# Zero products without pauses, and weight low parts on VectorE or GpSimd, in a two-layer hybrid backbone

## The chip, the cores and the metric

The kernel runs on one core of a Trainium2 chip. TensorE (PE) multiplies, VectorE (DVE), ScalarE (ACT) and GpSimd (POOL) do the elementwise work, and SyncE (SP) issues most transfers. The metric is the device time of one execution in microseconds: the median of several runs. Times below come from the runs and the profile of the kernel before.

## The reference

Two layers over 256 latent and 256 context tokens of width 1024, in fp32. Each layer: a modulated RMSNorm, one input projection for three mixers, a gated merge, an output projection, then a squared-ReLU MLP of width 4096. Cut to its core:

```python
for l in range(DEPTH):                       # DEPTH = 2
    sh1, sc1, g1, sh2, sc2, g2 = jnp.split(m_lat, 6, axis=-1)   # cond @ w_mod + b_mod
    h_lat = modulate(rmsnorm(x, norm1_g[l]), sh1, sc1)
    h_ctx = modulate(rmsnorm(ctx, norm1_g[l]), csh1, csc1)
    a_lat, a_ctx = parallel_mixer(h_lat, h_ctx, w_in[l], ...)   # GQA, neighbourhood, MLA
    x = x + g1 * a_lat
    x = x + g2 * sq_relu_mlp(modulate(rmsnorm(x, norm2_g[l]), sh2, sc2), w_mlp1[l], w_mlp2[l])
    if with_ctx:                             # layer 0 only
        ctx = ...                            # the same for the context tokens
return rmsnorm(x, final_norm_g)
```

In the mixer `ya`, `yb`, `yc` are softmax attentions over latent and context keys (8 heads of 64 each; the second with a 2-D window and a learned bias, the third with a low-rank key and a rotary part), and the merge is `(gates0 * (ya @ w_o_gqa) + gates1 * (yb @ w_o_na) + gates2 * (yc @ w_o_mla)) @ w_out`.

## The kernel before

**Split products.** Every fp32 product is three TensorE products of a reduced fp32 form: an operand a is split into hi (a cast on ScalarE, L723 for weights, L832 for activations) and lo = a - hi (a subtraction on VectorE, L724 and L833), and hi x hi + hi x lo + lo x hi goes into one PSUM bank (L786 to L788). A weight tile is 128 x 1024 fp32 (512 KB). Its fp32 form lands in a "raw" buffer (three of them, more while free slots are lent), ScalarE and VectorE write its pair wh, wl (three pairs, more when lent), and the raw buffer is given back when the low part is done. So a tile's low part sets when the next transfer into that buffer starts and when the third of its products may run. With 512 columns (layer 0: latent and context tokens) a tile carries 24 products of 512 columns, in layer 1 mostly 24 of 256.

**The order of the work.** While the program is built, a small event-driven planner plays it through. Each piece of work is a thread that asks for an engine with a cost, a lent buffer, an event or a sleep; each engine takes the waiting request with the lowest key, and the instruction is written into that engine's queue at that moment. An engine executes its queue in that order on the chip, waiting on semaphores. So the costs in the planner set only the order. The threads of the dense work come from a table of words (`SEQ`, one string a layer: `k0` is a weight tile of the keys, `gN2` a gate tile, `w` a tile of the modulation weights, `at` the square roots and rotations of the GQA queries and keys). The table also sets the order of the weight transfers. A request may name two engines ("any"); the first that is free takes it. `COLD` is the time up to which the planner doubles TensorE's costs and takes a longer transfer latency.

**The start.** The input is loaded, its squares are summed (ScalarE L983, VectorE L988), a product with ones gives the sums over channels (L1005), ScalarE takes the root (L1013), VectorE the reciprocal (L1014), a product spreads it over rows (L1026), and VectorE scales the input chunk by chunk (L1129). Meanwhile the conditioning weights arrive as sixteen tiles (c0 to c7, two halves each): four concurrent products of 32 columns a call (L859), a copy (L865), a sum over groups (L869) and two small VectorE steps (L876, L878). Then ScalarE modulates a chunk (L1137) and it is split (L832, L833).

**Attention.** Scores go to a bank, VectorE takes the row maximum (L1720, L1707), ScalarE the exponential (L1727), VectorE the reciprocal (L1739); the scaling is an "any" request of VectorE (L1738) and ScalarE (L1736); TensorE transposes (L1756), the result is split, and TensorE multiplies with the values (L1790, L1791). GpSimd issues the bias transfers (L1633) and clears and copies the rotary rows (L1463, L1469). Beside this the dense products of later tiles go on. The root of the GQA norms is L1524; the table for it and the table for the exponential are loaded in turn.

**Zeros.** `keep_warm` puts products of a zero tile (L914, 256 columns) into TensorE's queue where the planner sees TensorE idle.

Of the kernel before, what the change touches and what calls it, by code (L numbers as in the profile page):

```python
# [64 lines left out]

BR = {"N": NA, "L": ML, "G": GA}
SEQ = (
# [7 lines left out]
)  # L75


# [205 lines left out]
SL_W, SL_E, SL_G = 0.5, 10.0, 13.0  # L283
SL_M = 15.0
ANY = True
COLD = 9.0
IDLE = 0.08


# [247 lines left out]
def v_(n):  # L537
    return 0.07 + n * 0.00104
# [28 lines left out]
class Prog:  # L567
# [146 lines left out]
    def arrive(self, i, r, n):  # L714
        nc = self.nc
        yield from self.transfer(n)
        if self.keys[i][0] in ("mod", "modc"):
            self.raws[i] = r
            self.set("w", i)
            return  # L720
        pair = yield ("get", self.split, None)
        hi, lo = pair[0], pair[1]
        yield from self.act(n, lambda: nc.scalar.copy(hi[:, :n], r[0][:, :n]), SL_W)  # L723
        yield from self.dve(n, lambda: nc.vector.tensor_tensor(lo[:, :n], r[0][:, :n], hi[:, :n].bitcast(F32),  # L724
                                                               ALU.subtract), SL_W)
        self.give_raw(r)
        self.spl[i] = pair
        self.set("w", i)
# [177 lines left out]
    def keep_warm(self):  # L906

        nc, pl = self.nc, self.pl
        yield ("sleep", 2.0)
        while not self.ending and pl.now < 2000:  # L910
            if pl.busy["pe"] <= pl.now - IDLE and not pl.pend["pe"] and self.banks.free:
                def fn():
                    if self.banks.free:
                        nc.tensor.matmul(self.banks.free[0].ap[:, 0:256], self.zero,  # L914
                                         self.zero[:, 0:1].broadcast_to([P, 256]), start=True, stop=True)
                yield ("pe", 0.112, fn)
            else:
                yield ("sleep", 0.1)

    def cond_ready(self):  # L920
        yield ("sleep", 4.6)
# [716 lines left out]
    def attend(self, l, mine):  # L1638
        units = [(u, br, u % 4) for u, br in enumerate(b for b in BRANCHES for _ in range(4))]
        job = 0  # L1640
        for u, br, p in units:
            for e in sum(self.unit_needs(l, br, p), []):
                yield from self.wait(*e)
            yield from self.wait("ys", l, br)
            if u == 0:
                self.banks.caps.update(ATTN_CAPS)
                self.window.cap = WINDOW[1]
            kq, kv = self.unit_needs(l, br, p)
            groups = [(s, True) for s in range(2)] + ([(s, False) for s in range(2)] if l == 0 else [])
            nj = sum(2 if lat else 1 for s, lat in groups)  # L1650

            qleaf = []
            for e in kq:
                units_of = 4 if e[0] == "gak" else 1
                v = self.qk[e]
                if e not in self.leafs:
                    self.leafs[e] = Leaf(self, units_of * nj, [(self.arena, x) for x in v])
                qleaf.append(self.leafs[e])
            vleaf = []
            for e in kv:  # L1660
                if e not in self.leafs:
                    self.leafs[e] = Leaf(self, (4 if br == GA else 2) * len(groups), [(self.arena, self.vals[e])])
                vleaf.append(self.leafs[e])
            left = [len(groups)]
            for s, lat in groups:
                g = dict(u=u, br=br, p=p, s=s, lat=lat, n=2 if lat else 1, ready=Event(), got=Event(),
                         vleaf=vleaf, left=left)
                for qt in range(2 if lat else 1):
                    self.pl.spawn(self.job(l, g, qt, qleaf), job, -1)
                    job += 1  # L1670
                self.pl.spawn(self.pv(l, g), job - 0.5, -1)
        yield from self.wait("ydone", l, 11)
        self.free(*mine)
        self.banks.caps.update(DENSE_CAPS)
        self.window.cap = WINDOW[2]
        self.pl.serve(self.banks)
        self.pl.serve(self.window)
# [508 lines left out]
    def build(self, es):  # L2186
# [19 lines left out]
        self.wm_done, self.wm_total = 0, sum(i[0] == "wm" for i in self.items)  # L2206
        self.pl.busy["hw"] = 0.55
        self.pl.at(0.55, lambda: None)
        self.ending = False
        self.spawn(self.keep_warm(), 1 << 20, 9)  # L2210
        self.spawn(self.cond_ready(), 0)
        self.spawn(self.dense(), 0)
# [75 lines left out]
```

## Time and profile before

| | |
|---|---|
| median of 3 runs | 1442.91 us (1442.81 to 1444.1) |
| profiled execution | 1443.08 us, span 1441.3 us |
| busy: PE, DVE, ACT, POOL | 1417.8, 1074.0, 768.7, 52.9 us |
| granted TensorE clock | 0.994 of full, mean |
| transferred | 207.71 MB |
| zero products (L914) | 55 |

A line of the profile's groups reads: line, engine, operation, output <- inputs with their shapes, count, then busy time and mean length, then the idle time of that engine just before them and what ended it. A line of the order of time reads: start, length, engine, line, operation, names, count, and in brackets the idle time before it. A matmul's length overlaps the next one's, so TensorE counts as busy in the shadow of the last product too.

### The profile page before, as it was taken

How to read it: one execution, taken by the hardware profiler on the slowest of the kernel's cores; microseconds unless marked ns; L12 is line 12 of the kernel's file. 1: busy time of each engine (PE TensorE's matmuls, PEld its weight loads, DVE VectorE, ACT ScalarE, POOL GpSimd, SP SyncE). 2: the span in 40 equal slices, each digit the busy share in tenths (PEclk: the TensorE clock that was granted, in tenths of full speed). 3: DMA queues.
4: the chain of work that ended last, by engine and by line, in shares of the span. 5: the costliest groups of instructions: out<-in, count | busy, mean ns of one | idle time of the engine just before them, and what ended most of it. 6: DMA issues, size and time to landing. Idle time of an engine off the chain costs nothing.

```text
span 1441.3 us, 23357 instructions
## 1 busy us (share of the span) xinstructions
PE 1417.8 (98%) x8965; PEld 1268.1 (88%) x8965; DVE 1074.0 (75%) x2215; ACT 768.7 (53%) x1404; POOL 52.9 (4%) x91
## 2 busy tenths in 40 slices
PE   7999999999999999999999999999999999999997
PEld 4899889988888899888888889998998999999996
DVE  5638987859997779889867447657988997765555
ACT  6638886547842243413223234447779784554453
POOL 0000420000000000000000000000320000000000
PEclk8999999999999999999999999999999999999999
DMA  9501331413245444455655434334354427455551
GB/s 370 196 23 48 82 87 59 162 59 103 73 154 197 132 151 142 146 192 190 203 191 190 160 100 156 126 94 141 107 167 157 147 85 233 138 192 188 190 189 45
DMA packets 60528, 207.71 MB, mean 144 GB/s; under 512 B 7168, under 2 KB 8704, under 8 KB 60416
## 3 DMA queue, kind: packets, MB, share of 16 engines
q1 hardware_dynamic: 56448, 197.94, 41.3%
q0 software_dynamic: 2816, 6.82, 1.9%
q8 instruction: 70, 1.15, 0.3%
q10 hardware_dynamic: 1152, 1.45, 0.3%
q14 instruction: 42, 0.34, 0.1%
HBM read 201.47 MB, written 1.05 MB: 141 GB/s over the span
## 4 chain that ended last, share of the span: by engine, by line
PE 86%; DVE 7%; ACT 5%; DMA 1%; issue 1%; SPq 0%; DVEq 0%; ACTq 0%
PE b L786 25%; PE b L787 25%; PE b L788 25%; PE b L1756 2%; PE b L1791 2%; PE b L1790 2%; PE b L1584 1%; ACT s L1727 1%; PE b L1585 1%; DMA raw<-in_wts_dram 1%; ACT s L832 1%; DVE s L833 1%; DVE wl L724 1%; PE b L1760 1%; DVE s L943 1%
## 5 line engine op out<-in xcount | busy, mean ns | idle before, releaser
L786 PE MATMUL b<-s,wh 128*128 128x512 f32 (+1 forms) x1398 | 489.6, 350 | 0.0
L787 PE MATMUL b<-s,wh 128*128 128x512 f32 (+1 forms) x1398 | 484.3, 346 | 0.3 <-DVE s L1088 0.2
L788 PE MATMUL b<-s,wl 128*128 128x512 f32 (+1 forms) x1398 | 483.4, 346 | 0.1
L723 ACT CAST wh<-raw 128x1024 fp32r<-128x1024 f32 (+2 forms) x175 | 179.7, 1030 | 304.0 <-PE b L787 263.1
L788 PEld LDWEIGHTS b<-s,wl 128*128 128x128 f32 x1398 | 264.5, 189 | 33.2 <-DVE wl L724 0.3
L786 PEld LDWEIGHTS b<-s,wh 128*128 128x128 f32 x1398 | 264.7, 189 | 31.7 <-issue 0.8
L787 PEld LDWEIGHTS b<-s,wh 128*128 128x128 f32 x1398 | 264.8, 189 | 30.9 <-DVE s L1088 0.7
L724 DVE TENSOR_TENSOR wl<-raw,wh 128x1024 fp32r<-128x1024 f32 (+2 forms) x175 | 208.8, 1195 | 102.3 <-ACT wh L723 101.1
L786 PE MATMUL b<-s,s 128*128 128x256 f32 (+2 forms) x630 | 192.4, 305 | 0.5 <-ACT s L1087 0.3
L787 PE MATMUL b<-s,s 128*128 128x256 f32 (+2 forms) x630 | 190.4, 302 | 0.1
L788 PE MATMUL b<-s,s 128*128 128x256 f32 (+2 forms) x630 | 189.9, 301 | 0.0
L943 DVE CUSTOM_DVE_ANT_0 s<-raw,s 128x512 f32<-128x512 f32 x232 | 159.5, 687 | 16.1 <-DMA raw<-in_wts_dram 12.3
L786 PE MATMUL b<-wh,s 128*128 128x256 f32 (+2 forms) x436 | 132.6, 304 | 0.0
L787 PE MATMUL b<-wl,s 128*128 128x256 f32 (+2 forms) x436 | 131.2, 301 | 0.0
L788 PE MATMUL b<-wh,s 128*128 128x256 f32 (+2 forms) x436 | 131.2, 301 | 0.0
L786 PEld LDWEIGHTS b<-s,s 128*128 128x128 f32 x630 | 120.2, 191 | 4.4 <-ACT s L1087 0.6
L788 PEld LDWEIGHTS b<-s,s 128*128 128x128 f32 x630 | 120.1, 191 | 4.5 <-DVE s L724 0.2
L787 PEld LDWEIGHTS b<-s,s 128*128 128x128 f32 x630 | 120.3, 191 | 3.7 <-DVE s L1088 0.3
L833 DVE TENSOR_TENSOR s<-b,s 128x512 fp32r<-128x512 f32 (+2 forms) x143 | 95.0, 670 | 15.6 <-ACT s L832 14.7
L832 ACT CAST s<-b 128x512 fp32r<-128x512 f32 (+2 forms) x143 | 80.3, 577 | 19.3 <-PE b L1756 9.9
L724 DVE TENSOR_TENSOR wl<-s,wh 128x1024 fp32r<-128x1024 f32 x39 | 47.7, 1223 | 52.4 <-ACT wh L723 52.2
L786 PEld LDWEIGHTS b<-wh,s 128*128 128x128 f32 x436 | 83.1, 191 | 3.7
(174 smaller groups left out, 1994.0 us busy)
## 6 DMA issues: line engine op xcount, KB each, us to landing
raw<-in_wts_dram SPq DMA_DIRECT2D x291, 512.0 KB, 3.4
s<-in_wts_dram SPq DMA_DIRECT2D x69, 512.0 KB, 4.4
s<-in_xT_dram SPq DMA_DIRECT2D x16, 256.0 KB, 5.9
s<-in_bias_dram POOLq DMA_DIRECT2D x16, 192.0 KB, 2.7
s<-s POOLq DMA_DIRECT2D x24, 128.0 KB, 2.8
raw<-in_wts_dram SPq DMA_DIRECT2D x4, 384.0 KB, 3.5
s<-in_wts_dram SPq DMA_DIRECT2D x2, 432.0 KB, 5.4
raw<-in_wts_dram SPq DMA_DIRECT2D x2, 432.0 KB, 3.3
```

The source lines that it names most:

```text
L723: yield from self.act(n, lambda: nc.scalar.copy(hi[:, :n], r[0][:, :n]), SL_W)
L724: yield from self.dve(n, lambda: nc.vector.tensor_tensor(lo[:, :n], r[0][:, :n], hi[:, :n].bitcast(F32), ALU.subtract), SL_W)
L786: mm(out, a[0], b[0], start=start, stop=False)
L787: mm(out, a[0], b[1], start=False, stop=False)
L788: mm(out, a[1], b[0], start=False, stop=stop)
L832: yield from self.act(n, lambda: nc.scalar.copy(hi, src), slack)
L833: yield from self.dve(n, lambda: nc.vector.tensor_tensor(lo, src, hi.bitcast(F32), ALU.subtract), slack)
L943: yield ("dve", 0.73, lambda: nc.vector.tensor_tensor_reduce(self.junk, w[0][:, r], self.crow[j][:, r], 1.0, 0.0, ALU.mult, ALU.add, accum ...
L1584: mm(out, q[:, i], k[s][:, j], start=True, stop=False)
L1756: nc.tensor.transpose(ps[:, c * P:(c + 1) * P], pt[:, c * P:(c + 1) * P], self.ident)
L1790: mm(ps, v[o + k], hi[:, k, :], start=k == 0, stop=False)
L1791: mm(ps, v[o + k], lo[:, k, :], start=False, stop=k == nk - 1)
```

## The change

It has four parts. `keep_warm` issues zero products one behind another (cost 0.107, no poll between them) where it waited 0.08 after each; `COLD` goes from 9.0 to 5.2. While attention runs, a weight's low part is an "any" request of VectorE and GpSimd instead of VectorE's alone. And both strings of `SEQ` have another order. The diff, with two lines of the table:

```diff
 SEQ = (
-    "start c2 k0 more6 c3 c4 c7 c0 yL c1 raw5 k1 c6 c5 k2 q1 less w rope q0 ckv v0 q3 v1 q2 attn yN k3 l0 l1 gG7 "
+    "start c3 c0 c2 more6 k0 c7 c1 yL c4 k1 raw3 c6 q1 k2 c5 w rope less ckv q3 q0 v0 q2 attn yN v1 k3 l0 l1 l3 "
...
-    "l3 gL6 gG7 gN3 gG2 gN5 gL7 oN1 oN3 oL1 more2 at gN2 gL0 yG gL2 gN1 gN0 gL3 oN0 sN oG2 gL4 gN6 gG4 oL0 oN2 "
+    "l3 gN4 gN1 gN3 gL2 gG2 gN5 gL7 oN3 more2 gL6 oN1 gN2 gL3 at gL0 oL3 gL5 oG3 gG4 yG sN oN0 oL1 gG0 gN7 gN6 "
...
-COLD = 9.0
+COLD = 5.2
...
-        yield from self.dve(n, lambda: nc.vector.tensor_tensor(lo[:, :n], r[0][:, :n], hi[:, :n].bitcast(F32),
-                                                               ALU.subtract), SL_W)
+        def low(eng):
+            eng.tensor_tensor(lo[:, :n], r[0][:, :n], hi[:, :n].bitcast(F32), ALU.subtract)
+        if self.attending:
+
+            yield ("any", (("dve", v_(n), lambda: low(nc.vector)), ("pool", 0.1 + n * 0.0022, lambda: low(nc.gpsimd))), SL_W)
+        else:
+            yield from self.dve(n, lambda: low(nc.vector), SL_W)
...
     def keep_warm(self):
 
         nc, pl = self.nc, self.pl
-        yield ("sleep", 2.0)
+        yield ("sleep", 1.8)
+
+        def fn():
+            if self.banks.free:
+                nc.tensor.matmul(self.banks.free[0].ap[:, 0:256], self.zero,
+                                 self.zero[:, 0:1].broadcast_to([P, 256]), start=True, stop=True)
+        idle = IDLE
         while not self.ending and pl.now < 2000:
-            if pl.busy["pe"] <= pl.now - IDLE and not pl.pend["pe"] and self.banks.free:
-                def fn():
-                    if self.banks.free:
-                        nc.tensor.matmul(self.banks.free[0].ap[:, 0:256], self.zero,
-                                         self.zero[:, 0:1].broadcast_to([P, 256]), start=True, stop=True)
-                yield ("pe", 0.112, fn)
+            if pl.busy["pe"] <= pl.now - idle and not pl.pend["pe"] and self.banks.free:
+                yield ("pe", 0.107, fn)
+                idle = 0.0
             else:
                 yield ("sleep", 0.1)
+                idle = IDLE
...
             if u == 0:
+                self.attending = True
                 self.banks.caps.update(ATTN_CAPS)
...
         yield from self.wait("ydone", l, 11)
+        self.attending = False
```

In the changed kernel the lines of the steps named above are a few higher: zeros L918, conditioning products L864 and L874, sums L1014, broadcast L1035, reciprocal L1023, scaling L1138, low parts L725, root L1533, exponential L1738. The zero products are 152 where they were 55: 84 ahead of the first conditioning product (before 21), 34 in the rest of the start (before 20), 5 at two places after it (before 3), 29 around the second layer's second norm (before 10), and none at the very end (before 1). The products other than zeros are the same in number and shape.

In the following rows b_ is a PSUM bank, raw_ and s_ buffers (an s_ slot serves as raw buffer too), wh_ and wl_ a weight pair, rs_ the reciprocal root, mod_ modulation vectors. First TensorE near the start of the program, from the second conditioning group on. Before:

```order
L859 MATMUL b_75<-raw_67,s_112 32x256 x4
L1005 MATMUL b_76<-ones,s_113 128x1 x4
L869 MATMUL b_75<-sel,s_112 128x2 x2
L914 LDWEIGHTS zero
L914 MATMUL b_77<-zero 128x256
L859 MATMUL b_77<-s_141,s_112 32x256 x4
```

In the changed kernel, from the end of the 84 zeros on:

```order
L918 MATMUL b_76<-zero 128x256
L864 MATMUL b_75<-raw_66,s_112 32x256 x4
L1014 MATMUL b_76<-ones,s_113 128x1 x4
L864 MATMUL b_75<-raw_67,s_112 32x256 x4
L864 MATMUL b_77<-raw_68,s_112 32x256 x4
L1035 MATMUL b_78<-ident,rs_273 128x128 x4
L874 MATMUL b_75<-sel,s_112 128x2 x2
```

The sums stand behind one conditioning group instead of two, and the broadcast behind three groups and ahead of the first sum over groups; before, it came behind three groups, that sum and six zeros. VectorE at the same place, before:

```order
L988 TENSOR_TENSOR s_113<-s_113 128x512
L876 TENSOR_SCALAR mod_227<-b_75,bm_100,cc 128x2
L878 TENSOR_SCALAR mod_228<-b_75,cc 128x2
L724 TENSOR_TENSOR wl_70<-raw_68,wh_69 128x1024
L1014 RECIPROCAL rs_224<-rs_224 128x4
L1129 TENSOR_TENSOR s_108<-s_108,b_78 128x512 x2
```

and in the changed kernel:

```order
L997 TENSOR_TENSOR s_113<-s_113 128x512
L1023 RECIPROCAL rs_273<-rs_273 128x4
L1138 TENSOR_TENSOR s_108<-s_108,b_78 128x512
L881 TENSOR_SCALAR mod_294<-b_75,bm_100,cc 128x2
L883 TENSOR_SCALAR mod_295<-b_75,cc 128x2
L1138 TENSOR_TENSOR s_108<-s_108,b_78 128x512
```

The reciprocal follows the last sum of squares directly; the first weight's low part has moved behind all eight scalings.

Second, ScalarE in the second layer's attention (ss_ holds the sums of squares of the GQA norms). Before, the second of two visits to the root; the first, of 128x20, stands 17 rows earlier, with the same two table loads around it:

```order
L723 CAST wh_73<-raw_67 128x1024
L1524 ACT_TABLE_LOAD
L1524 ACTIVATE ss_9441<-ss_9441,eps 128x2x2
L832 CAST s_7791<-b_76 128x4x128
L1727 ACT_TABLE_LOAD
L1727 ACTIVATE s_6837,sm_9840<-b_81,sm_9840 128x512
```

In the changed kernel:

```order
L1533 ACT_TABLE_LOAD
L1533 ACTIVATE ss_9499<-ss_9499,eps 128x20
L837 CAST s_9559<-b_76 128x4x2x64
L723 CAST wh_71<-raw_66 128x1024
L1459 CAST s_9431<-b_78 64x512
L1459 CAST s_9557<-b_78 64x512
L837 CAST s_9560<-b_80 128x4x2x64
L1533 ACTIVATE ss_9499<-ss_9499,eps 128x2x2
```

Both roots now stand behind one table load, and the next table load (for L1850, a gate) comes six rows on, ahead of the next exponential. All in all ScalarE has 10 table loads where it had 12.

Third, GpSimd in the second layer's attention, between two groups of rotary rows. Before:

```order
L1469 DMA s_9131<-s_7785 32x1024
L1469 DMA s_9132<-s_7785 32x1024
L1463 MEMSET s_9352 32x2x256
L1463 MEMSET s_9353 32x2x256
L1463 MEMSET s_9354 32x1024
```

In the changed kernel:

```order
L1478 DMA s_9229<-s_7879 32x1024
L1478 DMA s_9230<-s_7879 32x1024
L725 TENSOR_TENSOR wl_74<-raw_66,wh_73 128x1024
L725 TENSOR_TENSOR wl_72<-raw_67,wh_71 128x768
L725 TENSOR_TENSOR wl_74<-raw_68,wh_73 128x1024
L1472 MEMSET s_9429 32x2x256
```

Three low parts stand in GpSimd's queue where none stood. In all 38 of the 278 low parts of weights are GpSimd's, 20 in the first layer's attention and 18 in the second's.

More of the change, by code (lines that the diff above doesn't have):

```diff
@@ L2208, in build @@
         self.pl.at(0.55, lambda: None)
-        self.ending = False
+        self.ending, self.attending = False, False
         self.spawn(self.keep_warm(), 1 << 20, 9)
```

10 rows, old and new, of the table SEQ are left out of this document.

## The prediction

> **What bounds the kernel now.** I read the page first (shares, then the chain of waits), then the busy time by stage, then the order of time in the stages where TensorE stands.
>
> ```profile
> PE 1417.8 (98%) x8965; PEld 1268.1 (88%) x8965; DVE 1074.0 (75%) x2215; ACT 768.7 (53%) x1404; POOL 52.9 (4%) x91
> PE 86%; DVE 7%; ACT 5%; DMA 1%; issue 1%; SPq 0%; DVEq 0%; ACTq 0%
> 0.00:34.00 34.00, 24.40 (x178) 13.83 (x179) 17.28 (x39) 19.79 (x36) 1.37 (x11) 0.80 0.96 369
> 109.00:405.00 296.00, 295.07 (x1850) 262.44 (x1849) 250.57 (x589) 216.10 (x477) 25.92 (x38) 1.00 0.29 92
> 405.00:967.00 562.00, 561.89 (x3161) 494.65 (x3160) 416.14 (x853) 196.80 (x296) 1.13 (x2) 1.00 0.48 156
> 967.00:1182.00 215.00, 210.81 (x1552) 197.17 (x1552) 189.42 (x436) 170.81 (x333) 23.26 (x38) 1.00 0.42 131
> 1430.00:1441.30 11.30, 3.86 (x18) 2.86 (x16) 7.38 (x16) 4.21 (x10) 0.00 (x0) 0.88 0.24 93
> ```
>
> Columns of the stage rows: stretch, its length, busy time (instructions) of PE, PEld, DVE, ACT, POOL, granted clock, DMA share, GB/s. The kernel is TensorE's: 86% of the chain is products, and 1441.3 - 1417.8 = 23.5 us is all its visible idle time. It lies in three places: 34 - 24.4 = 9.6 us at the start, 215 - 210.81 = 4.2 us in the second layer's attention, 11.3 - 3.86 = 7.4 us at the end. The first layer's attention holds 0.9 us, the dense stretch after it 0.1 us. The number of real products is the same in both kernels, so a gain can come from these places alone, and from the start, where even the busy time is partly zeros and half clock. The end is not touched.
>
> The start, by the order of time and by the granted clock:
>
> ```profile
> 1.59 4.16 PE L914 MATMUL b<-zero 128*128 128x256 bf16 x21 [1.59 <-POOL zero L2122]
> 11.55 1.08 PE L859 MATMUL b<-raw,s 128*32 128x256 f32 x8 [5.80 <-DMA raw<-in_wts_dram]
> 12.25 0.69 DVE L988 TENSOR_TENSOR s<-s 128x512 f32<-128x512 f32 x1 [0.98 <-ACT s L983]
> 14.33 1.87 PE L1005 MATMUL b<-ones,s 128*128 128x1 f32 x8
> 16.23 0.26 ACT L1013 ACTIVATE rs<-b,eps 128x4 f32<-128x4 f32 x1 [0.45 <-PE b L1005]
> 17.48 1.22 DVE L724 TENSOR_TENSOR wl<-raw,wh 128x1024 fp32r<-128x1024 f32 x1
> 18.62 0.17 DVE L1014 RECIPROCAL rs<-rs 128x4 f32<-128x4 f32 x1
> 18.84 2.07 PE L1026 MATMUL b<-ident,rs 128*128 128x128 f32 x8
> 20.95 1.88 DVE L1129 TENSOR_TENSOR s<-s,b 128x512 f32<-128x512 f32 x3 [2.17 <-PE b L1026]
> 22.87 1.09 ACT L1137 ACTIVATE s<-s,mod,mod 128x256 f32<-128x256 f32 x2 [0.50 <-DVE s L1129]
> 23.02 0.64 PE L859 MATMUL b<-s,s 128*32 128x256 f32 x8
> 33.47 0.48 PE L786 MATMUL b<-s,wh 128*128 128x512 f32 x1
> 5.75:8.50 2.75, 0.00 (x0) 0.00 (x0) 1.51 (x3) 1.33 (x3) 0.00 (x0) 1.00 0.99 338
> 8.50:11.52 3.02, 0.00 (x0) 0.00 (x0) 2.46 (x4) 2.89 (x5) 0.00 (x0) 0.50 1.01 403
> 11.52:22.20 10.68, 10.64 (x66) 6.09 (x66) 3.56 (x8) 2.48 (x6) 0.00 (x0) 0.50 1.03 411
> 22.20:34.00 11.80, 9.60 (x99) 4.90 (x92) 8.62 (x22) 10.34 (x21) 0.00 (x0) 1.00 1.03 409
> ```
>
> The 21 zeros end at 5.75, TensorE stands 5.8 us, the granted clock falls to 0.5 at 8.5 and comes back only near 22.2. In that half-clock stretch lies the chain that lets the dense work begin: the last sum of squares is done at 12.94; L1005 starts 1.4 us after it, behind conditioning products of 1.08 us a group (0.64 at full clock); the reciprocal waits behind L878 and the weight's low part L724 until 18.62, though its input was there at 16.5; L1026 takes 2.07 us. From 22.87 ScalarE is the pace (10.34 busy of 11.8), and the first dense product comes at 33.47.
>
> **The change part by part: the start.** The order now puts 84 zeros ahead of the first conditioning product, where 21 stood. A zero product at full clock is priced here:
>
> ```profile
> 1247.21 0.73 PE L914 MATMUL b<-zero 128*128 128x256 bf16 x5
> 1247.78 0.28 PE L1005 MATMUL b<-ones,s 128*128 128x1 f32 x2
> 1248.70 0.38 PE L1008 MATMUL b<-ones,s 128*128 128x1 f32 x2 [0.65 <-ACT s L983]
> 254.49 0.89 PE b L898 x8
> ```
>
> 1247.78 - 1247.21 = 0.57 us for five, 0.115 each. The first 21 cost 4.16 us again, the other 63 cost 63 x 0.115 = 7.2 us: the run ends at 1.59 + 4.16 + 7.2 = 12.95. That covers the wait for the first tile (11.55 before) with 1.4 us over, and it ends when the sums of squares are ready (12.94), so the overrun is hidden. The Trainium skill (TensorE: Matmul & The Clock Gate, Part 1: The HAM clock gate) says that about 3.4 us of steady activity releases the clock and one idle window of the same length takes it back. By that rule the clock stays full once it is up; the trace agrees, since 5.8 us without a product lost it at 8.5.
>
> At full clock, in the new order: one conditioning group 0.64 (to 13.6), the sums L1014 at the price of eight small full-clock products, 0.89 (the L898 row; to 14.5), ScalarE 0.26, the reciprocal 0.17, which now stands ahead of every other VectorE step there, and about 0.1 between engines: 15.0. TensorE has two more groups ahead of the broadcast (1.28, to 15.8), then 0.89: 16.7, against 18.84 + 2.07 = 20.9. The lead is 4.2 us. The first modulated chunk is now the one behind four L1129 steps of 0.63 (1.88 / 3) and two small ones, about 0.5: 16.7 + 2.5 + 0.5 = 19.7 against 22.87, so the lead at ScalarE is 3.2 us. The 34 zeros further on in the start stand where products wait for tiles; were none of that wait real, they would cost 34 x 0.115 = 3.9 us.
>
> What can eat the lead is the transfers, which run full (409 GB/s; 512 KB take 1.28 us). The last conditioning half moves from 18th to 20th tile, 2.6 us later; but two weight tiles come ahead of it and give work on seven of the eight chunks, and the dense products begin after five chunks' conditioning instead of six, one group and its two tiles earlier. I take **-3.5 us**: the 3.2 at ScalarE and a little of that last point. Bounds: -0.6 (the 2.6 us taken off the 3.2) and -5.5 (4.2 and one tile).
>
> **The second attention.** Half of its 4.2 us lies behind activation tables:
>
> ```profile
> 1090.69 1.28 ACT L1524 ACT_TABLE_LOAD   x1
> 1092.32 1.28 ACT L1727 ACT_TABLE_LOAD   x1
> 1103.06 1.28 ACT L1524 ACT_TABLE_LOAD   x1
> 1105.14 1.28 ACT L1727 ACT_TABLE_LOAD   x1
> 1095.25 0.63 PE L1756 MATMUL b<-ident,s 128*128 128x128 f32 x4 [0.99 <-DVE sm L1739]
> 1107.27 0.38 PE L1790 MATMUL b<-s,s 128*128 128x256 f32 x1 [0.73 <-ACT s L1727]
> 1110.69 0.50 PE L786 MATMUL b<-s,s 128*128 128x512 f32 x1 [0.17 <-ACT s L1727]
> ```
>
> The square roots of the two norms visited ScalarE at two times, each with a load of the root's table and of the exponential's again. In the new order both roots stand in one visit: two loads of 1.28 go. The waits right behind the second visit, 0.73 + 0.17 = 0.9 us, go with them; of the 0.99 behind the first I count half, since no exponential now stands right behind the root: **-1.4 us**, between 0 (another chain is late there) and -1.9.
>
> **Low parts on GpSimd.** 38 of 278 go: 20 in the first layer's attention, 18 in the second's.
>
> ```profile
> L724 DVE TENSOR_TENSOR wl<-raw,wh 128x1024 fp32r<-128x1024 f32 x31 | 37.7, 1219 | 4.6 <-ACT wh L723 4.4
> L1738 DVE TENSOR_SCALAR s<-s,sm 128x512 f32<-128x512 f32 x30 | 15.3, 510 | 0.5
> L1463 POOL MEMSET s<- 32x1024 f32 x24 | 23.0, 960 | 29.8 <-PE b L1791 15.3 <-PE b L1585 7.8 <-PE b L788 3.9
> masks.py:199 POOL TENSOR_SCALAR_AFFINE_SELECT ident<-ident 128x128 f32<-128x128 f32 x1 | 0.3, 287 | 0.1
> masks.py:197 POOL MEMSET ident<- 128x128 f32 x1 | 0.2, 204 | 0.3 <-POOLq L2276 0.3
> ```
>
> VectorE loses 18 x 1.22 = 22 us of its 189.4 in the 215 us of the second attention. No GpSimd subtraction is in the trace. Writing 1024 elements took it 0.96 us; reading one input added 287 - 204 = 83 ns for 128, so two inputs of 1024 add up to 16 x 83 ns = 1.33: an estimate of 2.3 us, between 0.96 and twice the estimate, 4.6. A low part is then 1.1 us later than on a free VectorE. Three weight pairs cover that: a tile's 24 products at 210.81 / 1552 = 0.136 us give 3.3 us of work. The Trainium skill (GPSIMD Engine Reference, 3.1 Elementwise) measured 4497 ns for 2048 elements, by which one here would be about 2.25 us, an estimate; the sum would not move. Behind these steps on GpSimd's queue stand the bias transfers and the rope memsets; GpSimd goes from 23.3 busy to about 65 of the 215 us, so its queue is mostly empty and I cost that at nothing; without that cover each one caught behind a low part is 2.3 us late. I take **-0.5 us** for a freer VectorE (its rows end most of the remaining waits), between -2.3 (what is left of the 4.2) and +10 (second rival).
>
> **The last norm.** 19 zeros stand before its sums, where five stood: 19 x 0.115 = 2.2 us against the 1248.70 - 1247.21 = 1.5 us that the step waited anyway: **+0.4 us**, between 0 and +0.7. The rest of the table moves dense work within stretches that are full; I put it at nothing, and at 1.5 us either way in the range.
>
> Sum: 1443.08 (the profiled execution, 1441.3 of span and 1.8 around it) - 3.5 - 1.4 - 0.5 + 0.4 = **1438.1 us**. The median, 1442.91, is 0.2 below that execution: 1438.0.
>
> **Rivals.** (1) The start is paced by transfers and by ScalarE, so the clock is worth 0.6, and new waits in attention take the rest: 1441 to 1444. For it: DMA 0.99 to 1.03 busy until 34. Against it: tiles lie ready while the chain at 18.6 waits for VectorE.
>
> (2) Slower: GpSimd and VectorE shut each other out. If VectorE's steps with two inputs in SBUF stand while GpSimd reads, each of the 18 holds it up to 2.3 us: 41 us, while 22 are freed, so VectorE goes from 189.4 to 208.8 of 215 and becomes the bound. Half of those 19.4 us on TensorE is 10: 1443 - 3.5 + 10 = about 1449. It decides from about 1.2 us held up for each, where what is freed is used up. For it: L724 itself is the commonest such step, and not all of the 31 in its row above go. Against it: most other steps there read PSUM, and GpSimd's memsets leave no mark on VectorE. The Trainium skill (SBUF — State Buffer, Who interferes with whom) states just such a lock, for the whole instruction; no row here shows it, as GpSimd read next to nothing.
>
> (3) More: all of the 4.2 us in attention goes and the start gives its upper bound: 1443 - 4.2 - 5.5 = 1433.
>
> (4) The change doesn't do what it says: the zeros fail to hold the clock. Then the chain keeps only the reciprocal's place (18.62 against 16.5, 2 us): 1441. It is in the chance of (1).
>
> **How the numbers follow.** Forecast 0.53, (1) and (4) 0.20, (2) 0.12, (3) 0.15. About 0.2% (2.9 us, 1440.0 to 1445.8) is what this measurement can tell from no change. Of the forecast 0.08 lies above 1440, and of (1) and (4), whose low end touches it, 0.12: faster 0.45 + 0.15 + 0.08 = 0.68; same 0.08 + 0.12 = 0.20; slower 0.12. The range is 1432 to 1444: it takes in (1) and (3) and leaves out (2) and a tail below. The forecast's own is 1435 to 1441.
>
> **What would show it.** Right: a granted clock of 1.00 from 5 to 34 us, the broadcast's end near 16.7, the first dense product near 30, one visit to the root's table in the second attention, GpSimd's low parts at 2 to 2.6 us and L724 on VectorE still at 1.22. Wrong: a first dense product after 32; VectorE's two-input steps stretched to 2 us or more; waits of TensorE in the second attention above 4.2 us; weights' low parts as what ends them.

## The result, and the profile after

The changed kernel took 1477.26 us (median; 1474.12 to 1479.08), the kernel before 1442.86 (1442.79 to 1444.1) beside it: a ratio of 1.0226, 95% interval 1.0208 to 1.0244. It is 34 us slower. The page of the changed kernel, its busy shares, its chain of waits, and then the busy time by stage, with columns as in the prediction:

```profile
PE 1430.8 (97%) x9062; PEld 1278.5 (87%) x9062; DVE 1087.0 (74%) x2190; ACT 760.1 (52%) x1389; POOL 144.5 (10%) x129
PE 75%; DVE 17%; DMA 3%; ACT 3%; issue 1%; SPq 0%; DVEq 0%; ACTq 0%
...
0.00:34.00 34.00, 30.80 (x280) 20.69 (x281) 19.36 (x41) 21.66 (x40) 1.38 (x11) 1.00 0.96 367
109.00:405.00 296.00, 282.93 (x1767) 248.39 (x1766) 251.32 (x570) 202.04 (x448) 69.03 (x57) 1.00 0.27 87
405.00:967.00 562.00, 559.95 (x3119) 490.94 (x3118) 416.92 (x851) 196.88 (x299) 5.29 (x4) 1.00 0.48 157
967.00:1182.00 215.00, 196.95 (x1403) 184.00 (x1402) 171.50 (x379) 149.40 (x296) 60.27 (x53) 0.98 0.39 121
```

The chain now runs over VectorE for 17% of the span, where it was 7%. TensorE is less full in the two attentions: idle 13 us of 296 (0.9 before) and 18 us of 215 (4.2 before). VectorE's total busy time rose, 1087.0 for 1074.0, although 38 subtractions of 1.22 us left it. It isn't full in any of these stages: 171.5 of 215 us.

What TensorE waited for, over the whole span (columns: total, times, longest, in us):

```profile
PE b L1767 <- DVE s L1749: 15.9, 11, 4.2
PE b L1767 <- DVE s L838: 5.7, 3, 2.0
PE b L1802 <- DVE s L838: 4.6, 6, 1.3
```

The transposes (L1767) wait for the scaling of the probabilities (L1749). That line and the product with raw modulation weights (L952), by source line, with shortest, median and longest in ns: the changed kernel, and the same two lines (L1738, L943) of the kernel before.

```profile
L1749 DVE TENSOR_SCALAR s<-s,sm x95: 331/481/2690, 112.5 to 1200.4; 128x512 f32<-128x512 f32 x63, 128x256 f32<-128x256 f32 x32
L952 DVE CUSTOM_DVE_ANT_0 s<-raw,s x244: 659/691/2807, 258.2 to 1097.3; 128x512 f32<-128x512 f32 x122
```

```profile
L1738 DVE TENSOR_SCALAR s<-s,sm x86: 334/478/1071, 113.9 to 1180.0; 128x512 f32<-128x512 f32 x58, 128x256 f32<-128x256 f32 x28
L943 DVE CUSTOM_DVE_ANT_0 s<-raw,s x232: 666/691/695, 266.8 to 1076.8; 128x512 f32<-128x512 f32 x116
```

The medians are unchanged; the longest is 2.5 times as long for the scaling and four times for the product. The kernel before has a small mark of the same kind: its longest scaling, 1071 ns, and its second longest run beside GpSimd's memsets.

```profile
1021.66 0.83 DVE L1738 TENSOR_SCALAR s<-s,sm 128x512 f32<-128x512 f32 x1
1022.60 1.07 DVE L1738 TENSOR_SCALAR s<-s,sm 128x512 f32<-128x512 f32 x1
...
1021.12 3.43 POOL L1463 MEMSET s<- 32x512 f32 x4
```

Steps that read a PSUM bank show nothing of it. In the changed kernel, the same line L838 with its two kinds of input, the row maximum, and then GpSimd's new group:

```profile
L838 DVE TENSOR_TENSOR s<-b,s x143: 406/681/694, 75.3 to 1202.7; 128x512 fp32r<-128x512 f32 x136, 128x256 fp32r<-128x256 f32 x4, 32x256 fp32r<-32x256 f32 x2, 32x512 fp32r<-32x512 f32 x1
L838 DVE TENSOR_TENSOR s<-s,s x48: 405/682/2666, 24.1 to 1260.7; 128x512 fp32r<-128x512 f32 x28, 128x256 fp32r<-128x256 f32 x20
L1731 DVE TENSOR_REDUCE sm<-b x64: 661/681/695, 181.2 to 1198.7; 128x1 f32<-128x512 f32 x64
...
L725 POOL TENSOR_TENSOR wl<-raw,wh 128x1024 fp32r<-128x1024 f32 x30 | 73.8, 2459 | 261.8 <-ACT wh L723 233.3 <-PE b L1767 19.7 <-issue 6.6
```

One such place in order of time (second attention; VectorE, GpSimd, TensorE), and the stage row behind it:

```profile
1077.29 0.67 DVE L952 CUSTOM_DVE_ANT_0 s<-raw,s 128x512 f32<-128x512 f32 x1
1077.89 2.56 DVE L1749 TENSOR_SCALAR s<-s,sm 128x512 f32<-128x512 f32 x1
...
1077.54 2.63 POOL L725 TENSOR_TENSOR wl<-raw,wh 128x1024 fp32r<-128x1024 f32 x1 [13.34 <-ACT wh L723]
...
1076.07 0.28 PE L793 MATMUL b<-wh,s 128*128 128x256 f32 x1
1080.50 1.12 PE L1767 MATMUL b<-ident,s 128*128 128x128 f32 x4 [4.16 <-DVE s L1749]
...
1080.50:1086.00 5.50, 5.50 (x23) 5.21 (x24) 3.38 (x9) 2.80 (x6) 0.00 (x0) 0.50 0.53 163
```

GpSimd's subtraction runs from 1077.54 to 1080.17. The scaling, ordinarily 0.48 us, starts inside it and ends at 1080.45, 0.28 us after GpSimd: it stood for 2.1 us and then ran. TensorE, which had come to the end of what it could do at 1076.35, stands 4.16 us where an estimate without the hold is 4.16 - 2.1 = 2.1, and the granted clock is 0.50 for the next 5.5 us.

I compared every VectorE instruction that overlaps a GpSimd subtraction with the median of its own kind elsewhere in this trace. 25 of the 38 subtractions held one, by 0.3 to 2.2 us; together 47.4 us (L1749 15.1, L952 13.5, the rest steps of other lines with operands in SBUF), 1.25 us for each of the 38. Some 25 us of it lie in the first layer's attention and 22 in the second's. Steps reading PSUM in the same places are longer by some 14 ns at most.

To place the loss I use TensorE's lost time by stage: from each product's start to the next, less the spacing of full stretches (0.227 us for 512 columns, 0.120 for 256, 0.109 for 128), zeros counted as lost, half clock too. The real products are the same 1392.1 us in all kernels. A row of the table is one profiled execution; "order" is the new table of words.

| kernel | 0-34 | 34-405 | 405-967 | 967-1300 | sum |
|---|---|---|---|---|---|
| before | 21.5 | 5.1 | 1.7 | 12.7 | 41.5 |
| changed | 18.4 | 21.2 | 4.8 | 31.0 | 75.8 |
| e1: changed, all low parts on VectorE | 18.0 | 6.2 | 4.3 | 19.2 | 47.9 |
| e2: before + "any" low parts | 21.3 | 21.2 | 2.7 | 29.5 | 75.2 |
| e3: before + zeros | 18.2 | 5.0 | 1.6 | 13.8 | 39.0 |
| e4: before + order | 20.6 | 7.8 | 3.6 | 15.6 | 48.0 |
| e11: before + first row of the order | 21.7 | 7.6 | 2.0 | 12.4 | 43.9 |
| e5: changed, GpSimd only writes | 18.4 | 9.0 | 3.1 | 11.8 | 42.4 |
| e9: changed, GpSimd reads one tensor | 18.4 | 13.4 | 2.8 | 17.8 | 52.7 |
| e6: changed, its 38 moved to VectorE, same order | 18.0 | 15.1 | 5.7 | 23.0 | 62.1 |
| e7: changed, scaling in another form | 18.4 | 20.1 | 3.8 | 29.7 | 72.4 |
| e12: e3 + both roots in one request | 18.2 | 5.1 | 1.9 | 11.2 | 36.7 |
| e10: e12, fewer zeros at the last norm | 18.6 | 5.0 | 1.6 | 10.6 | 35.9 |

(What lies behind 1300 us is 0.1 to 0.6.) Of the 34.3 us that the changed kernel lost, 16.1 lie in the first layer before 405 us, 3.1 in the dense stretch, 18.3 in the second layer, and the start gained 3.1.

### The profile page after: what moved, and what is told of

Same layout as the page of the kernel before. It is cut to its first block, busy times and chain, and to the rows that moved or that the text cites. A ratio compares the mean times of both kernels' runs of the same rounds, so it can differ in the third digit from the quotient of the medians.

```text
span 1475.9 us, 23524 instructions
## 1 busy us (share of the span) xinstructions
PE 1430.8 (97%) x9062; PEld 1278.5 (87%) x9062; DVE 1087.0 (74%) x2190; ACT 760.1 (52%) x1389; POOL 144.5 (10%) x129
## 4 chain that ended last, share of the span: by engine, by line
PE 75%; DVE 17%; DMA 3%; ACT 3%; issue 1%; SPq 0%; DVEq 0%; ACTq 0%
PE b L791 23%; PE b L792 23%; PE b L793 23%; DMA raw<-in_wts_dram 2%; DVE s L838 2%; DVE s L952 2%; DVE s L1749 2%; PE b L1767 2%; DVE sm L1731 1%; PE b L1802 1%; DVE wl L725 1%; PE b L1801 1%; ACT s L1738 1%; PE b L1593 1%; DVE s L1811 1%
## 5 line engine op out<-in xcount | busy, mean ns | idle before, releaser
L723 ACT CAST wh<-raw 128x1024 fp32r<-128x1024 f32 (+3 forms) x184 | 189.0, 1030 | 320.5 <-PE b L792 266.7
L725 DVE TENSOR_TENSOR wl<-raw,wh 128x1024 fp32r<-128x1024 f32 (+3 forms) x151 | 181.1, 1201 | 121.0 <-ACT wh L723 117.5
L791 PE MATMUL b<-s,s 128*128 128x256 f32 (+2 forms) x658 | 199.1, 303 | 0.0
L793 PE MATMUL b<-s,s 128*128 128x256 f32 (+2 forms) x658 | 197.0, 299 | 0.3 <-DVE s L1097 0.3
L792 PE MATMUL b<-s,s 128*128 128x256 f32 (+2 forms) x658 | 197.2, 300 | 0.0
L952 DVE CUSTOM_DVE_ANT_0 s<-raw,s 128x512 f32<-128x512 f32 x244 | 175.6, 720 | 16.2 <-DMA raw<-in_wts_dram 12.2
L793 PEld LDWEIGHTS b<-s,s 128*128 128x128 f32 x658 | 125.8, 191 | 4.4 <-DVE s L1097 0.5
L791 PEld LDWEIGHTS b<-s,s 128*128 128x128 f32 x658 | 125.9, 191 | 3.3
L792 PEld LDWEIGHTS b<-s,s 128*128 128x128 f32 x658 | 126.0, 191 | 3.2
L791 PE MATMUL b<-wh,s 128*128 128x256 f32 (+2 forms) x408 | 125.9, 309 | 0.0
L792 PE MATMUL b<-wl,s 128*128 128x256 f32 (+2 forms) x408 | 124.2, 304 | 0.0
L793 PE MATMUL b<-wh,s 128*128 128x256 f32 (+2 forms) x408 | 124.0, 304 | 0.0
L725 POOL TENSOR_TENSOR wl<-raw,wh 128x1024 fp32r<-128x1024 f32 (+2 forms) x33 | 78.5, 2379 | 284.5 <-ACT wh L723 250.2
L838 DVE TENSOR_TENSOR s<-b,s 128x512 fp32r<-128x512 f32 (+2 forms) x143 | 94.7, 670 | 14.8 <-ACT s L837 13.8
L1738 ACT ACTIVATE s<-b,sm 128x512 f32<-128x512 f32 (+1 forms) x112 | 66.8, 600 | 32.0 <-DVE sm L1731 28.1
```

Of the source, the lines that this page charges most:

```text
L725: eng.tensor_tensor(lo[:, :n], r[0][:, :n], hi[:, :n].bitcast(F32), ALU.subtract)
L791: mm(out, a[0], b[0], start=start, stop=False)
L792: mm(out, a[0], b[1], start=False, stop=False)
L793: mm(out, a[1], b[0], start=False, stop=stop)
L838: yield from self.dve(n, lambda: nc.vector.tensor_tensor(lo, src, hi.bitcast(F32), ALU.subtract), slack)
L952: yield ("dve", 0.73, lambda: nc.vector.tensor_tensor_reduce(self.junk, w[0][:, r], self.crow[j][:, r], 1.0, 0.0, ALU.mult, ALU.add, accum ...
```

## The experiments

**The parts one by one.** e1 is the changed kernel without the "any" request, e2 the kernel before with that request alone, e3 with the zeros alone (and `COLD`), e4 with the table of words alone.

```diff
 # e1, on the changed kernel; e2 puts the change's lines for the low parts into the kernel before
-        if self.attending:
+        if False:
```

> The changed kernel with every low part on VectorE again; zeros and table of the order as changed (the planner lays the rest out anew). Theory L (GpSimd's subtraction holds VectorE's steps that read two inputs in SBUF, and the scaling of the probabilities): the two attentions go back to about 1 and 4 us of TensorE waits, the start keeps its gain: 1437 to 1441 us. Theory O (the new table of the order is what the chip can't follow): it stays at 1465 or more. Theory Z (zeros and the planner's earlier warm clock put the order wrong): also 1465 or more.

> The kernel before with only the low parts on VectorE or GpSimd during attention. L: slower than before by about what attention lost in the changed kernel, 25 to 40 us: 1468 to 1483. O and Z: within a few us of before, 1438 to 1448.

> The kernel before with only the zeros without pauses and the planner's earlier full clock. L: the start gains 2 to 4 us and nothing is lost: 1438 to 1441. Z: slower than before by 10 or more. O: 1438 to 1443.

> The kernel before with only the new table of the order. L: within 4 us of before, 1439 to 1447 (its start is laid for another clock). O: 1460 or more. Z: as L.

Measured: e1 1448.52 (1447.31 to 1450.14; ratio 1.0030, 1.0016 to 1.0043). e2 1478.28 (1475.88 to 1480.14; 1.0236, 1.0218 to 1.0254). e3 1441.37 (1439.99 to 1444.8; 0.9985, 0.9976 to 0.9995). e4 1449.15 (1446.04 to 1450.17; 1.0031, 1.0018 to 1.0044). So the "any" request alone does all of the damage, +35; the zeros alone gain about 2; and the order alone, which I had at nothing, costs about 6, the miss of e1 and e4 against the expectation. e1 and e3 differ by the table of words alone, and there it costs 7. The planner lays the work out anew in each of these kernels: e1 has 12 table loads again. So the parts do not add up: 35 + 6 - 2 = 39 us for 34.

**Is it the reading?** e5 leaves the 38 on GpSimd at the same places of all orders, but lets GpSimd write instead of read.

```diff
-            eng.tensor_tensor(lo[:, :n], r[0][:, :n], hi[:, :n].bitcast(F32), ALU.subtract)
+            m = n if eng is nc.vector else 16
+            eng.tensor_tensor(lo[:, :m], r[0][:, :m], hi[:, :m].bitcast(F32), ALU.subtract)
+            if m < n:
+                for c0 in (16, 16, n // 2):
+                    eng.memset(lo[:, c0:n].bitcast(F32), 0.0)
```

> The changed kernel, with the same 38 low parts given to GpSimd at the same places, but there GpSimd subtracts only the first 16 columns and then fills the rest of the tile with zeros three times over (twice n-16 columns and once n/2): about the same time on GpSimd (2.4 us instead of 2.46, an estimate), nearly without reading. Left out is the low part of those 38 tiles beyond column 16, so the output is less exact. Theory H (while GpSimd's subtraction reads, VectorE's instructions with operands in SBUF alone are held until it ends): VectorE's instructions beside GpSimd go back to their own lengths (the two-input step of L952 to 0.69 us, the scaling of L1749 to 0.48), the 47 us of stretch fall to under 10, and the time falls to 1437 to 1447 us. Rival Q (the low part is ready later by GpSimd than by VectorE, 2.46 for 1.22 us, and what waits for the low part is late): nothing of this changes, 1472 to 1480 us. Rival P (any work of GpSimd on SBUF, writes as well, holds VectorE): 1472 to 1480 us too, but with the stretch in place.

Measured: 1444.96 us (1444.05 to 1448.92), 1.001 (1.0001 to 1.002). By stage, then the waits, then the scaling and the modulation step; lines are four higher there (transposes L1771, scaling L1753, modulation L956):

```profile
109.00:405.00 296.00, 293.19 (x1838) 259.40 (x1838) 241.33 (x594) 209.36 (x466) 77.58 (x118) 1.00 0.29 97
967.00:1182.00 215.00, 210.68 (x1568) 198.94 (x1567) 179.00 (x431) 167.67 (x333) 72.33 (x110) 1.00 0.40 131
...
PE b L1771 <- DVE s L1753: 3.7, 5, 1.5
...
L1753 DVE TENSOR_SCALAR s<-s,sm x95: 334/485/1411, 112.7 to 1167.1; 128x512 f32<-128x512 f32 x63, 128x256 f32<-128x256 f32 x32
L956 DVE CUSTOM_DVE_ANT_0 s<-raw,s x244: 660/691/696, 254.8 to 1074.3; 128x512 f32<-128x512 f32 x122
```

GpSimd is busier than in the changed kernel (77.58 and 72.33 us for 69.03 and 60.27), and its part of a full tile takes even longer (0.28 + 2 x 0.97 + 0.55 = 2.8 us by its groups), yet 32 of the 34 us are gone. VectorE's stretch beside the low parts falls from 47.4 to some 7 us; what is left, 12 holds of 0.3 to 0.9 us, sits on the scaling and a cast, none on the two-input steps, 62 of which ran beside GpSimd. (The expectation of e9 below reckons with 1.7 us and "held nobody"; the trace shows these 7.) The lateness of the low parts (rival Q) is out, and GpSimd's writes as such (rival P) hold too little for the price.

**How much of GpSimd's reading?** e9 lets GpSimd read one tensor instead of two.

```diff
-            eng.tensor_tensor(lo[:, :n], r[0][:, :n], hi[:, :n].bitcast(F32), ALU.subtract)
+            if eng is nc.vector: return eng.tensor_tensor(lo[:, :n], r[0][:, :n], hi[:, :n].bitcast(F32), ALU.subtract)
+            for c0 in (0, 16): eng.tensor_scalar(lo[:, c0:n], r[0][:, c0:n], 0.0, None, ALU.mult)
```

> The changed kernel, same order, with the 38 low parts on GpSimd worked out from one tensor in place of two: the weights times 0, twice over, so that GpSimd still reads 1024 columns in SBUF while it writes. Left out is the low part of those 38 tiles (zeros stand there), so the output is less exact. GpSimd's fills alone (no reading) held nobody: 1445.0 us, 1.7 us of stretch on VectorE. Theory R (any reading by GpSimd in SBUF holds VectorE): the stretch of VectorE's steps stays at 35 us or more over the 38 and the time at 1465 to 1480 us. Theory T (only GpSimd's instructions with two tensors as input hold it): the stretch falls to under 8 us, and the time to 1443 to 1450 us.

Measured: 1455.22 us (1453.4 to 1456.84), 1.0076 (1.0056 to 1.0095), between the two.

```profile
L726 POOL TENSOR_SCALAR wl<-raw 128x1024 fp32r<-128x1024 f32 x30 | 86.3, 2877 | 158.4 <-PE b L793 77.3 <-PE b L792 49.2 <-DMA raw<-in_wts_dram 15.8
...
L952 DVE CUSTOM_DVE_ANT_0 s<-raw,s x244: 660/691/1471, 255.3 to 1081.4; 128x512 f32<-128x512 f32 x122
```

Neither theory holds as written. The one-input step took longer than the subtraction (2.88 for 2.46 us), so GpSimd worked 211 us where it had worked 91. In these 211 us VectorE was stretched by some 23 us over 36 steps, never by more than 0.9 us at once, and in most of them the held step ends well inside GpSimd's instruction. Half of it, 12 us, lies on the scaling and a cast, which fills hold too; the other half on steps with two SBUF inputs, which no fill held (L952: longest 1471 ns here, 696 in e5). So one-input reading holds VectorE too, but for a part of the instruction. Why only a part wasn't tried.

**Which steps are held?** e7 gives the scaling a form of VectorE's instruction that also writes an accumulator column.

```diff
-                    nc.vector.tensor_scalar(pt[:, r], pt[:, r], sm[:, 2 + a:3 + a], None, ALU.mult)
+                    nc.vector.tensor_scalar(pt[:, r], pt[:, r], sm[:, 2 + a:3 + a], None, ALU.mult, ALU.max,
+                                            accum_out=sm[:, 4 + a:5 + a])
```

> The changed kernel, same order, with the scaling of the probabilities (L1749, 95 times) in the form that also writes a sum column: longer each time (0.7 instead of 0.48 us, an estimate from the other steps of VectorE that have one) but the same result. Theory H-a (what is held at L1749 is the form of VectorE's that moves several elements in a cycle; the slower form is not held): the scaling's longest falls from 2.69 us to under 1.0, its 15 us of stretch vanish, the waits of TensorE for it (15.9 us in the stretch of the first attention) fall to under 6, and the time falls to 1460 to 1470 us. Rival H-b (whatever VectorE reads and writes in SBUF is held): the longest stays at 2.5 us or more, and the time rises to 1478 to 1490 us by 95 times 0.2 us of longer work.

Measured: 1476.98 us (1474.27 to 1479.33), 1.0228 (1.0209 to 1.0247), the same time as the changed kernel.

```profile
L1749 DVE TENSOR_SCALAR_CACHE_REDUCE s<-s,sm x95: 459/737/748, 112.6 to 1197.0; 128x512 f32<-128x512 f32 x63, 128x256 f32<-128x256 f32 x32
...
PE b L1768 <- DVE s L1749: 14.6, 8, 3.9
```

On the mechanism H-a is right: the longest is 0.748, not one of 95 is held, though 17 of them ran beside a subtraction. On the time it is wrong: the transposes (L1768 there) wait 14.6 us for the scaling where they waited 15.9 (both over the whole span). Each scaling is 0.13 (256 columns) to 0.26 us longer, some 20 us of VectorE; that this took up the gain is likely but not shown. The Trainium skill (SBUF — State Buffer, Who interferes with whom) says which VectorE instructions take the pair of ports that it shares with GpSimd: those in a two-port mode, which this scaling can enter but not the form with an accumulator, and, against a GpSimd instruction that reads, those with two SBUF inputs. e5 (fills hold the scaling, no two-input step) and e7 agree with both halves; e9's short holds do not fit its "for the whole instruction".

**The amount or the place?** e6 keeps the changed kernel's orders and puts the 38 subtractions back on VectorE, unplanned.

```diff
-            ... ("pool", 0.1 + n * 0.0022, lambda: low(nc.gpsimd))), SL_W)
+            ... ("pool", 0.1 + n * 0.0022, lambda: low(nc.vector))), SL_W)
```

> The changed kernel, with the order of TensorE, ScalarE and the transfers kept to the instruction, and the 38 subtractions that GpSimd had put on VectorE at the same places of its order, 1.22 us each, 46 us that this order had not reckoned with. It asks whether it matters who fills VectorE. Theory H1 (the price comes from VectorE being late by 1.2 us again and again in an order that gave it no time for that): nearly the same lateness, 1465 to 1480 us. Theory H2 (the price comes from where the holds fall, on the scaling of the probabilities and the two-input steps that products wait for, and not from the amount): the same 46 us at the low parts' own places, ahead of no product that waits, cost less, 1445 to 1460 us.

Measured: 1463.18 us (1461.62 to 1465.15), 1.0134 (1.0118 to 1.0149). Stage, waits, and the modulation step:

```profile
967.00:1182.00 215.00, 202.39 (x1465) 188.13 (x1463) 181.58 (x424) 160.27 (x318) 23.19 (x38) 1.00 0.37 122
...
PE b L1767 <- DVE s L1749: 10.3, 11, 3.0
...
L952 DVE CUSTOM_DVE_ANT_0 s<-raw,s x244: 659/691/696, 255.7 to 1087.0; 128x512 f32<-128x512 f32 x122
```

The result lies between the two theories. No step is held by a subtraction, VectorE gets 45 us in pieces of 1.22, and TensorE loses 62.1 - 42.4 = 20 us against e5. The changed kernel puts 47 us there in pieces of about 2 and loses 33. So lateness of VectorE without such holds is enough for some 60% of the price, in an order that had given its time away (e5 isn't free of holds, so both losses are lower bounds). The other 13.7 us belong to what sets the holds apart, longer single pieces at other places; of these, by an estimate, 4 us are the clock, which stays at 1.00 in e6's second attention and is at 0.98 of 215 us in the changed kernel. The rest I did not separate.

**The order.** e11 is the kernel before with the first row alone of the new table.

> The kernel before with the first row alone of the new table of words (the order of the work up to the second layer); the second row, the zeros and the low parts stay as before. The whole new table alone gave 1449.15, 5.7 us over before, of which by the lost time of TensorE some 4 us lay before 967 us and 3 behind it. If the two rows cost each by itself: 1446 to 1448. If the first row is good alone and the two only fail together (the second was ordered for what the first leaves): 1442 to 1444.

Measured: 1447.14 us (1444.71 to 1447.99), 1.0016 (1.0007 to 1.0025): about 3 of the order's 6. They lie between 34 and 405 us by the table (7.6 lost for 5.1), but not all are the order's own: with the old zeros e11 runs at a clock of 0.50 once more from 25.4 to 28.8 us and e4 from 33.6 to 36.9, which the changed kernel doesn't. By difference with e4 the second row costs about as much behind 967. With GpSimd writing only (e5) the second layer is at 11.8, better than before, but the first attention stays at 9.0; e1, with the same table and no low part on GpSimd, is at 6.2. Which step of the first row it is remains open.

**What is worth keeping.** The zeros of e3, with the saved table loads made for certain by asking both roots in one request (e8, and again as e12), and with the pauses kept at the last norm (e10).

```diff
-        for r in ([ss[:, :, :]] if l == 0 else [ss[:, 0:2, :], ss[:, 2:4, 8:10]]):
-            yield ("act", 1.5, lambda: nc.scalar.activation(r, r, AF.Sqrt, bias=self.eps, scale=1.0 / 64), SL_G)
-            yield ("dve", 0.3, lambda: nc.vector.reciprocal(r, r), SL_G)
+        rs = [ss[:, :, :]] if l == 0 else [ss[:, 0:2, :], ss[:, 2:4, 8:10]]
+        yield ("act", 1.5, lambda: [nc.scalar.activation(r, r, AF.Sqrt, ...) for r in rs], SL_G)
+        yield ("dve", 0.3 * len(rs), lambda: [nc.vector.reciprocal(r, r) for r in rs], SL_G)
 # e10, in keep_warm
-                idle = 0.0
+                idle = 0.0 if pl.now < 1100 else IDLE
```

> The kernel before with the change to the zeros alone, and with both square roots of the second layer's rotation norms asked of ScalarE in one request, so that they stand next to each other and their pair of table loads is saved (10 loads for 12); low parts and table of words stay as before. The zeros alone gave 1441.4. If the saved loads are on the path in the second attention, as the prediction had it (1.4 us): 1439.5 to 1440.5. If they lie beside other work: 1441 to 1442, the same as the zeros alone.

> The zeros and the single request for both roots on the order of the kernel before, once more, as the partner of the run without zeros at the last norm and for a firmer ratio: 1439.1 us as before, 0.997 of the kernel before.

> The zeros and the single request for both roots, on the order of the kernel before, with the zeros of the last norm laid with pauses again (10 or so in place of 29); the start as in the changed kernel. If the row of 19 zeros at the last norm (2.3 us) stands ahead of work that could start: 0.5 to 1.5 us faster than with them, 1437.6 to 1438.6. If the norm sets the time there and the zeros only fill its gap: the same, 1438.8 to 1439.4.

Measured: e8 1439.13 us (1438.46 to 1439.53), 0.9967 (0.9954 to 0.998); e12 1438.66 (1438.35 to 1439.14), 0.996 (0.9947 to 0.9973); e10 1438.01 (1437.38 to 1438.98), 0.9956 (0.9943 to 0.9969). e10 beats both kernels of this case, by 5.8 us the one before. The loads of the root's table fall from three to two; the last norm in e12 and then in e10:

```profile
1241.85 2.28 PE L913 MATMUL b<-zero 128*128 128x256 bf16 x19
1243.97 0.28 PE L1009 MATMUL b<-ones,s 128*128 128x1 f32 x2
...
1247.70 0.38 PE L786 MATMUL b<-s,wh 128*128 128x256 f32 x1
```

```profile
1241.85 0.84 PE L913 MATMUL b<-zero 128*128 128x256 bf16 x6
1242.53 0.28 PE L1009 MATMUL b<-ones,s 128*128 128x1 f32 x2
...
1246.95 0.38 PE L786 MATMUL b<-s,wh 128*128 128x256 f32 x1
```

Both start at 1241.85; behind 19 zeros the dense products come back at 1247.70, behind 6 at 1246.95, 0.75 us earlier. The executions' ranges overlap, so for the whole time those 0.65 us aren't settled; for the place they are.

## Why the prediction was wrong

**The start: right.** The changed kernel in order of time (TensorE, ScalarE and VectorE together):

```profile
1.60 10.90 PE L918 MATMUL b<-zero 128*128 128x256 bf16 x84 [1.60 <-POOL zero L2133]
12.99 1.05 PE L1014 MATMUL b<-ones,s 128*128 128x1 f32 x8
14.38 0.18 DVE L1023 RECIPROCAL rs<-rs 128x4 f32<-128x4 f32 x1 [1.80 <-ACT rs L1022]
14.98 1.16 PE L1035 MATMUL b<-ident,rs 128*128 128x128 f32 x8
19.88 1.59 ACT L1146 ACTIVATE s<-s,mod,mod 128x256 f32<-128x256 f32 x3
26.34 0.50 PE L791 MATMUL b<-s,wh 128*128 128x512 f32 x1
31.60 0.50 PE L791 MATMUL b<-s,wh 128*128 128x512 f32 x1
```

The zeros end at 12.50 (12.95 predicted), the clock stays at 1.00 from 4.6 us to the end of the stage, the broadcast ends at 16.14 (16.7), the first modulated chunk starts at 19.88 (19.7). The dense products start at 31.60 with a single earlier tile at 26.34, where I had "near 30". The stage loses 3.1 us less in the changed kernel and 3.3 in e3, for 3.5. In the stand from 1076.35 the granted clock fell to half about 3.4 us on, near 1079.75 (the row from 1079.00 to 1080.50 has 0.75 in the mean). The Trainium skill's rule (TensorE: Matmul & The Clock Gate, Part 1: The HAM clock gate), that an idle window of about 3.4 us halves the clock, agrees with that stand. As a threshold it isn't sharp here: e1 ran at 0.50 behind a stand of 2.64 us from 1095.67, and the changed kernel kept its clock behind one of 2.82 us from 340.83. Rivals 1 and 4 fall.

**The second attention's table loads: right in kind.** Both roots stand in one visit. Under the holds this can't be seen in the changed kernel; in e8 and e12, without them, the second layer loses 12.6 and 11.2 us for 13.8 in e3: 1.2 and 2.6 for 1.4. These are two executions of one kernel, so the size is known no better than that.

**The last norm: +0.4 predicted, 0.7 measured**, the upper bound: the 19 zeros stand ahead of work that could start.

**The rest of the table, "at nothing": wrong.** It costs about 6 us alone (e4), and about as much with the low parts on VectorE (e1). My bound was 1.5. I had argued that dense work moves within full stretches; but those stretches are full because the old order fed them, and the prediction rests on no row of the two orders between 34 and 405 us.

**Low parts on GpSimd, -0.5 with +10 as its worst: the step that failed.** The mechanism was the second rival's, and its sign in the profile came as named: two-input steps of 2 us and more, waits of TensorE above 4.2 us. The length of a low part on GpSimd came out as estimated (2.46 us for 2.3), and the rival's threshold was met too, 1.25 us held for each low part against 1.2. Three things in that rival were wrong.

First its chance, 0.12. I set "most other steps there read PSUM" and "GpSimd's memsets leave no mark" against it. The first is true of the counts and useless: it was enough that a GpSimd instruction of 2.5 us meets one step of the exposed kinds, and 25 of 38 did. The second is not quite true: two scalings of the kernel before stand beside memsets at 0.83 and 1.07 us for 0.48, and they make the mean of 510 ns in the prediction's own row. It also says little of reading, as e5 shows: fills hold VectorE for some 7 us in all, and putting them in place of the reading takes away 32 us of the time. Nor had I counted the scaling among the exposed steps, since only one of its inputs is a tensor; it was the one that TensorE waited for.

Second its price, 10 us. I worked it as load: held time less freed time, as if VectorE had to become the bound. By load this kernel should have lost nothing, 47 us held for about 45 freed, and VectorE stays at 171.5 of 215 us. The price is lateness on a chain (maximum, exponential, reciprocal, scaling, transpose) for which TensorE waits. e5 against the changed kernel is that price: 75.8 - 42.4 = 33 us of TensorE, 0.9 us for every low part. e6 shows that 45 us of late VectorE time cost 20 us without any hold by a low part.

Third its place. The rival reckoned with the 18 low parts of the second attention alone; the 20 of the first had no price at all. There 25 of the 47 us are held, and TensorE loses 16 of the 34 us before 405.

Had GpSimd's reading held nobody, the change would still have missed the forecast: e5's 1445.0 is 7 above it, about the order's price, though the fills' holds lie in it too; rival 3's 1433 was out of reach with it.

## What to carry to other kernels

Before giving work to GpSimd, list what VectorE runs beside it by kind of operand: steps with two SBUF inputs and fast one-input steps from SBUF to SBUF were held here while GpSimd read two tensors there, the fast one-input steps for a shorter time by its fills too, and steps that read PSUM were not. Price a hold by who waits behind the held step, not by VectorE's share: at 80% busy, 47 us of holds cost 33 us, and 20 of these came without such holds as well, in an order that had given that time away. And keep an order of work out of the "costs nothing" column when parts of it are planned on the assumption that fails; here its own 6 us were hidden under the larger loss.

## What was not expected of the hardware

- GpSimd's one-input step (weights times 0, 128 x 1024) took 2.88 us, longer than its two-input subtraction with 2.46, and three times its fill with 0.97. It held VectorE for at most 0.9 us at a time, the subtraction for up to 2.2, to its own end.
- GpSimd's fills held VectorE's scaling and cast by up to 0.9 us (e5), and no two-input step.
- The same scaling on VectorE is 0.48 us and can be held to 2.69, or 0.74 us and isn't held, by whether it also writes an accumulator.
- A hold of 2.1 us can cost more than itself: it lies in a stand of TensorE of 4.16 us in which the granted clock halved, and 5.5 us at 0.50 followed.
